# The mixer's last 512 output columns by token block in banks of their own, and routing's subtractions and the give-back matrix placed elsewhere

## The chip, the cores and the metric

One Trainium2 chip, one core. The metric is the device time of one execution in microseconds. A trace of one profiled execution is at hand; its times are counted from the start of its span. Engines: PE is TensorE (PEld its weight loads), DVE is VectorE, ACT is ScalarE, POOL is GpSimd, SP is SyncE, which here issues transfers only.

## The reference

Two blocks on 256 tokens of 1024 features, all in fp32. The first is a gated linear attention with a convolutional feed-forward. The second, where the change lies, is a token mixer (sparse attention and a gated delta rule, merged, times `w_out`), a layer norm, a mixture of 32 experts in 4 groups of 8, and a second layer norm:

```python
x = layer_norm(alpha * x + (1.0 + gt1) * y, ln_g[l, 0], ln_b[l, 0])   # y = merged @ w_out
h = x * (1.0 + sc2) + sh2
y = hier_moe(h, w_route_grp[l], w_route_exp[l], w_gate[l], w_up[l], w_down[l])
x = layer_norm(alpha * x + (1.0 + gt2) * y, ln_g[l, 1], ln_b[l, 1])

# hier_moe: the best group, in it the two best experts of 8
hb = silu(xb @ w_gate[e]) * (xb @ w_up[e])
yb = (hb @ w_down[e]) * gate
```

## The kernel before, in words

All instructions are put on the five engines' queues by a scheduler that goes by the order in which the program names them and by when they are ready in its own model; each queue then runs in order. `tc.issue_after(i)` holds what is named under it behind instruction i on i's engine.

*The mixer's output product* is `linA(xsm, w_out, ..., sink_o, tail=TAIL, fine=FINE)`. It makes two halves of 512 output columns, `ct` 0 and 1, each from four weight tiles of 256 rows. Each tile is loaded (`raw`), its high part is written by ScalarE (L177, `whi`), its low part by VectorE (L178, `wlo`); `mm3` makes three matmuls of each product (L187 to L189). With `tail=1` a tile is used for both token blocks (`tb`) of 128 as it comes. With `fine=2` the last tile of the last half is used in two steps of 256 columns for each token block. `sink_o` scales a finished piece and adds the residual (L1334, L1335), takes its statistics (L1337), and later transposes it on PE (L1343, L1344) for the routing logits (L1347); these two steps are queued behind the newest mixer matmul at that time. The slots `raw`, `lo` and `hi` (6, 4 and 4 of them) are used again for expert weights.

*Routing* is `route(tb)` for each token block: mean and scale from the statistics (`lstat`, with a power on GpSimd, L295), normalised rows `n3` and their high part `n3h` on ScalarE (L1388, L1389), and on VectorE the logits and the selection (L1383 to L1403, result `sel`), four subtractions for the low part `n3l` (L1405, one per token block and half), and the position of each token in its expert's list from a count on PE (L1410, `pos`, L1411). `onehots` compares positions (L1416, `dm`); `pick` multiplies `n3h` and `n3l` with it on PE (L1424, eight feature blocks `ff`), which collects the tokens of four experts in four banks. `gather(g)` moves these to `xg` (L1503 on VectorE, L1505 on ScalarE), then makes the gates (`gates`, L1463 to L1481), transposes `dm` to `cT` and sums each slot's gate in `gs`; these two, the give-back matrix and scale, are used when an expert's result is added to its tokens. An overflow count `nov` (L1532 to L1540) follows.

*The experts* run in 16 pairs. For each pair `gate_up` makes 64 matmuls (gate, then up), SiLU and product on ScalarE and VectorE (L1608, L1609), `turn` transposes the result, and `down` of the pair before makes 32 matmuls and gives the result back with `cT`. These matmuls go through `inorder`, which keeps them in program order on PE; a helper's line stands for all of them, L1424. `spread` (L435) makes broadcast rows on PE; those for the sums of the experts and for their scale are named in the second pair and are not held in order.

*Expert weights* are pieces of 1 MB, or of two halves, in the order of `plist`, each with a slot fixed beforehand (`cyc`); SP issues them in order (L1210), each when its slot is free. 18 pieces are named ahead of routing.

Of the kernel before, what the change touches and what calls it, by code (L numbers as in the profile page):

```python
# [9 lines left out]
F32 = mybir.dt.float32  # L10
# [11 lines left out]
CAP = 64  # L22
# [73 lines left out]
def _build(ctx, tc, nc, I, out, dbg):  # L96
# [15 lines left out]
    def bank(pool_=None, name="bank"):  # L112
        p = ps if pool_ is None else pool_
        return p.tile([128, 512], F32, tag="b", name=name)
# [71 lines left out]
    def mm3(o, ah, al, bh, bl, start, stop, **kw):  # L186
        pe.matmul(o, lhsT=ah, rhs=bh, start=start, stop=False, **kw)  # L187
        pe.matmul(o, lhsT=ah, rhs=bl, start=False, stop=False, **kw)  # L188
        mm_last[0] = pe.matmul(o, lhsT=al, rhs=bh, start=False, stop=stop, **kw).ins  # L189
# [18 lines left out]
    def linA_(xs, w, K, c0, sink, head=1, tail=1, fine=1):  # L208


        xh, xl = xs
        KT = K // 128
        for ct in range(2):
            p = [bank(pm) for _ in range(2)]

            def part(tb, k0, kn, hi, lo, cs=slice(0, 512)):
                ts = slice(tb * 128, (tb + 1) * 128)
                for k in range(kn):
                    kk = k0 + k
                    mm3(p[tb][:, cs], xh[:, kk, ts], xl[:, kk, ts], hi[:, k, cs], lo[:, k, cs], kk == 0, kk == KT - 1, skip_group_check=fine > 1)  # L220

            held = []
            tiles = [(k0, 2) for k0 in range(0, KT, 2)]
            for i, (k0, kn) in enumerate(tiles):
                held.append((k0, kn) + wload(kslice(w, k0, kn, c0 + ct * 512, 512), kn, 512))
                last = i == len(tiles) - 1
                if not last and (i < head - 1 and ct == 0 or i >= len(tiles) - tail and ct == 1):
                    yield
                    continue
                n = fine if last and ct == 1 else 1  # L230
                for tb in range(2):
                    for c in range(n):
                        cs = slice(c * 512 // n, (c + 1) * 512 // n)
                        for t in held:
                            part(tb, *t, cs)
                        if last and fine == 1:
                            sink(ct, tb, p[tb])
                        elif last:
                            sink(ct * 512 + cs.start, tb, p[tb][:, cs])
                held = []  # L240
                yield

# [42 lines left out]
                                          op1=ALU.subtract)  # L285
        return ia.ins, iv.ins

    pow_last = [None]

    def rsqrt(ms, eps, n):  # L290

        a = smp.tile([128, n], F32, tag="rs_a", name="rs_a")
        r = smp.tile([128, n], F32, tag="rs_r", name="rs_r")
        dve.tensor_scalar(out=a, in0=ms, scalar1=eps, scalar2=None, op0=ALU.add)  # L294
        pool.tensor_tensor(out=r, in0=a, in1=mhalf[:, :n], op=ALU.pow)  # L295
        return r

    def junk():
# [293 lines left out]
    with tc.tile_pool(reuse_waits="tile", name="ffn", bufs=2) as fp:  # L592
# [43 lines left out]
        for i in range(11):  # L636
            gu = {}

            def sink(nm, cw, cb):
                def f(ct, p):  # L640
                    o = fp.tile([128, 2, 256], F32, tag=nm, name=nm)
                    for c in range(2):
                        conv(p, c, i * 2 + c, cw, cb, o[:, c])
                    gu[nm] = o
                return f
# [669 lines left out]
    def mt(shape, name):  # L1315
        return mp.tile([128] + list(shape), F32, name=name, bufs=1)
# [41 lines left out]
    def lstat(st):  # L1358
        mvv = smp.tile([128, 2], F32, tag="bnmv", name="bnmv")
        dve.bn_aggr(out=mvv, in_=st)  # L1360
        return mvv[:, 0:1], rsqrt(mvv[:, 1:2], 1e-5, 1)
# [13 lines left out]
    n3h, n3l = (xtile(i, F32R, nm, (2, 2, 4, 128)) for i, nm in ((1, "n3h"), (2, "n3l")))  # L1375
    pkq = lambda ap: ap.rearrange("p (c k) -> p k c", k=4)

    def route(tb):
        m, r = lstat(lst[tb])
        nm = smp.tile([128, 1], F32, tag="nm", name="nm")  # L1380
        dve.scalar_tensor_tensor(out=nm, in0=m, scalar=-1.0, in1=r, op0=ALU.mult, op1=ALU.mult)
        l = lg[:, tb]
        dve.scalar_tensor_tensor(out=l, in0=wst[:, 0], scalar=nm, in1=wst[:, 1], op0=ALU.mult, op1=ALU.add)  # L1383
        with ExitStack():
            dve.scalar_tensor_tensor(out=l, in0=plg[tb][:, 0:36], scalar=r, in1=l, op0=ALU.mult, op1=ALU.add)

        for q, cs in enumerate(halves):
            act.activation(out=n3[:, tb, cs], in_=v3[:, tb, cs], func=AF.Identity, scale=r, bias=nm)  # L1388
            act.activation(out=n3h[:, tb, q], in_=pkq(n3[:, tb, cs]), func=AF.Copy)  # L1389

        kg, e = kg_[:, tb], el[:, tb]
        dve.tensor_reduce(out=mg_[:, tb:tb + 1], in_=l[:, 0:4], op=ALU.max, axis=AX)
        dve.scalar_tensor_tensor(out=kg, in0=l[:, 0:4], scalar=mg_[:, tb:tb + 1], in1=C("io4"), op0=ALU.is_ge, op1=ALU.mult)
        dve.tensor_reduce(out=kx[:, tb:tb + 1], in_=kg, op=ALU.max, axis=AX)
        dve.tensor_scalar(out=kg, in0=kg, scalar1=kx[:, tb:tb + 1], scalar2=-BIG, op0=ALU.is_lt, op1=ALU.mult)
        dve.tensor_tensor(out=e.rearrange("p (g e) -> p g e", g=4), in0=l[:, 4:36].rearrange("p (g e) -> p g e", g=4),
                          in1=kg[:, :, None].to_broadcast([128, 4, 8]), op=ALU.add)

        dve.max(out=m8[:, tb], in_=e)
        dve.scalar_tensor_tensor(out=ke[:, tb], in0=e, scalar=m8[:, tb, 1:2], in1=C("io32"), op0=ALU.is_ge, op1=ALU.mult)  # L1400
        dve.scalar_tensor_tensor(out=ke[:, tb], in0=e, scalar=m8[:, tb, 1:2], in1=ke[:, tb], op0=ALU.is_gt, op1=ALU.add)
        dve.max(out=k8[:, tb], in_=ke[:, tb])
        sel_last[0] = dve.tensor_scalar(out=sel[:, tb], in0=ke[:, tb], scalar1=k8[:, tb, 1:2], scalar2=None, op0=ALU.is_ge).ins  # L1403
        for q, cs in enumerate(halves):
            dve.tensor_tensor(out=n3l[:, tb, q], in0=pkq(n3[:, tb, cs]), in1=n3h[:, tb, q].bitcast(F32), op=ALU.subtract)  # L1405

        p = bank()
        if tb:
            pe.matmul(p[:, 0:32], lhsT=C("ones"), rhs=sel[:, 0], start=True, stop=False)
        i = pe.matmul(p[:, 0:32], lhsT=C("lall"), rhs=sel[:, tb], start=tb == 0, stop=True)  # L1410
        dve.scalar_tensor_tensor(out=pos[:, tb], in0=sel[:, tb], scalar=-1000.0, in1=p[:, 0:32], op0=ALU.mult, op1=ALU.add)  # L1411
        return i.ins
# [32 lines left out]
    picked = [bank(pm) for _ in range(4)]  # L1445
    route(0)
    onehots(0, 0)
    for ff in range(4):
        pick(pk(picked, ff), 0, ff, 0)
    with tc.issue_after(route(1)):  # L1450
        for ff in range(4, 8):
            pick(pk(picked, ff), 0, ff, 0)
    idm = onehots(0, 1)
    for ff in range(8):
        pick(pk(picked, ff), 0, ff, 1)

# [27 lines left out]
    def gather(g):  # L1484

        if g:
            dms[g] = dtile_()
            for tb in range(2):
                onehots(g, tb)
        dm = dms[g]  # L1490
        xg = mp.tile([128, 8, 256], F32, tag="xg", name="xg", bufs=1)
        for ff in range(8):

# [9 lines left out]
                dve.tensor_scalar(out=xg[:, ff], in0=pv, scalar1=g_, scalar2=b_, op0=ALU.mult, op1=ALU.add)  # L1503
            else:
                act.activation(out=xg[:, ff], in_=pv, func=AF.Identity, scale=g_, bias=b_)  # L1505
        if g == 0:
            with tc.issue_after(idm):
                gates()
        p, pg = bank(), bank()
        pv = p.rearrange("p (q t c) -> p q t c", q=2, t=2)  # L1510
        pgv = pg[:, 0:8].rearrange("p (q h e) -> p q e h", q=2, h=2)
# [11 lines left out]
        for e in range(2):  # L1523
            es = slice(e * 64, e * 64 + 64)
            dve.tensor_reduce(out=gs[es], in_=pgv[es, :, e], op=ALU.add, axis=AX)
        return xg, cT, gs

    NP = NE // 2
    xg, cT, gs = gather(0)

    gov = ke
    dve.tensor_scalar(out=gov, in0=pos, scalar1=CAP - 1000.0, scalar2=None, op0=ALU.is_ge)  # L1532
    dve.tensor_tensor(out=gov, in0=gov, in1=sel, op=ALU.mult)
    nov = mt([1], "nov")
    dve.tensor_reduce(out=nov, in_=gov.rearrange("p t e -> p (t e)"), op=ALU.add, axis=AX)
    p = bank()
    pe.matmul(p[0:1, 0:2], lhsT=nov, rhs=C("ones")[:, 0:2], start=True, stop=True)
    novi = mp.tile([1, 1], I32, name="novi", bufs=1)
    dve.tensor_copy(out=novi, in_=p[0:1, 0:1])
    dve.tensor_tensor(out=gov, in0=gov, in1=Gm, op=ALU.mult)  # L1540
    normT = mp.tile([16, 128], F32, name="normT", bufs=1)
    pool.dma_start(out=normT, in_=I["rows"][3072:5120].rearrange("(q c) -> q c", q=16))

    def overflow():

        def wdyn(src):
# [99 lines left out]
    def down_last(pr, hT, cT, gs):  # L1646
# [8 lines left out]
        for c in range(4):  # L1655
# [3 lines left out]
            for tb in range(2):  # L1659
                yq = yps[tb][c // 2][:, s]  # L1660
                inorder(pe.matmul, yq, lhsT=cT[:, q, tb].bitcast(F32), rhs=ye, start=False, stop=True, skip_group_check=True)
                dve.bn_stats(out=fst[tb][:, c], in_=yq)  # L1662


    todo = None
    started.append(1)
    for pr in range(NP):
        last = pr == NP - 1
        while cnt[0] < ahead[pr]:
            wpiece()  # L1670
        hs_, back = gate_up(pr, xg), (cT, gs)
        if pr == NP - 2:

            lgb = xtile(1, name="lgb", shape=(2, 1024))
            for n in range(2):
                spread_to(lgb[:, n], normT, n)
        if pr % 2 and not last:
            xg, cT, gs = gather(pr // 2 + 1)
        if pr == 1:

            yps = [[bank(pm) for _ in range(2)] for _ in range(2)]
# [45 lines left out]
RA, RB = 5, 2  # L1727
TA, TB = 1, 2
BA, AHD = (0, 2), 3
TAIL, ZH, FP_, ZP_, NB0, NB1, FINE = 1, 2, 3, 3, 10, 15, 2  # L1730

def pack(inputs):
    g = lambda n: np.asarray(inputs[n])
# [42 lines left out]
```

## Time and profile before

| | |
|---|---|
| median of three executions | 1190.06 us (1189.28 to 1191.07) |
| the profiled execution | 1189.94 us |
| its span | 1188.3 us |
| busy: PE, DVE, ACT, POOL | 1138.7, 639.2, 457.9, 56.1 us |
| from HBM | 333.12 MB read, 283 GB/s over the span |

Busy times are sums over the span; stages differ much, and PE counts as busy while its matmuls are pipelined. Start times in a timeline are of the profiled execution, in us from the span's start; a line with xN merges N instructions.

### The profile page before, as it was taken

What the parts mean: (1) busy time and instruction counts of PE and PEld (TensorE: products, weight loads), DVE (VectorE), ACT (ScalarE), POOL (GpSimd) and SP (SyncE); (2) the same over time, 40 slices, a digit from 0 to 9 for tenths busy, and PEclk for the clock granted to TensorE, in tenths of its full rate; (3) what the DMA queues carried; (4) which work ended last, traced back from release to release, by engine and by line L of the source; (5) the groups of instructions that cost most, each with busy time, mean ns of one, the idle gap of its engine ahead of it and who ended that gap; (6) DMA issues with size and microseconds to landing.
All of it is one profiled execution on the core that took longest, in us unless ns stands there. A gap on an engine that the chain in (4) does not pass through costs nothing. (4 is left out here: it accounts for less than half of the span.)

```text
span 1188.3 us, 17092 instructions
## 1 busy us (share of the span) xinstructions
PE 1138.7 (96%) x6642; PEld 806.3 (68%) x6642; DVE 639.2 (54%) x1109; ACT 457.9 (39%) x827; POOL 56.1 (5%) x76
## 2 busy tenths in 40 slices
PE   6999999999999999999999989999999799999986
PEld 5976799998778999989988765534443334434432
DVE  5797788998887899487467562212121112211104
ACT  5654566664566666453365431201010101101100
POOL 1001100000010111100100000000000000000000
PEclk9999999999999999999999989999999899999998
DMA  9884787778954647345356875999999999999992
GB/s 328 276 313 151 244 297 225 222 238 294 324 178 141 178 125 202 105 127 136 115 226 222 308 273 219 373 420 416 417 421 417 415 419 417 419 419 417 420 414 99
DMA packets 136262, 337.69 MB, mean 284 GB/s; under 512 B 12891, under 2 KB 69415, under 8 KB 121328
## 3 DMA queue, kind: packets, MB, share of 16 engines
q1 hardware_dynamic: 126160, 328.83, 75.1%
q0 software_dynamic: 1696, 5.36, 1.2%
q10 hardware_dynamic: 8320, 2.36, 0.8%
q8 instruction: 54, 0.88, 0.3%
q14 instruction: 32, 0.26, 0.1%
HBM read 333.12 MB, written 3.32 MB: 283 GB/s over the span
## 5 line engine op out<-in xcount | busy, mean ns | idle before, releaser
L178 DVE TENSOR_TENSOR wlo<-raw,whi 128x1024 fp32r<-128x1024 f32 (+1 forms) x192 | 234.0, 1222 | 81.3 <-ACT whi L177 80.4
L177 ACT ACTIVATE whi<-raw 128x1024 fp32r<-128x1024 f32 (+1 forms) x192 | 201.2, 1052 | 177.9 <-PE bank L188 65.0
L1424 PE MATMUL bank<-wmoe,xg 128*64 128x512 f32 x1024 | 233.3, 600 | 6.5 <-PEq L1553 6.1
L188 PE MATMUL bank<-xl,whi 128*128 128x256 f32 x720 | 204.6, 284 | 0.3 <-DVE xl L284 0.3
L187 PE MATMUL bank<-xh,whi 128*128 128x256 f32 x720 | 204.8, 284 | 0.0
L189 PE MATMUL bank<-xh,wlo 128*128 128x256 f32 x720 | 204.4, 284 | 0.0
L1424 PEld LDWEIGHTS bank<-wmoe,xg 128*64 128x64 f32 x1024 | 72.8, 138 | 145.3 <-issue 139.4
L188 PEld LDWEIGHTS bank<-xl,whi 128*128 128x128 f32 x720 | 137.9, 192 | 1.6 <-DVE xl L284 0.5
L187 PEld LDWEIGHTS bank<-xh,whi 128*128 128x128 f32 x720 | 138.0, 192 | 1.5 <-ACT whi L177 0.5
L189 PEld LDWEIGHTS bank<-xh,wlo 128*128 128x128 f32 x720 | 137.9, 192 | 0.9 <-issue 0.8
L1609 DVE TENSOR_TENSOR hsT<-hsT,bank 128x512 f32<-128x512 f32 x16 | 11.0, 688 | 230.7 <-PE bank L1424 217.8
L1424 PE MATMUL bank<-wmoe,hsT 128*64 128x512 f32 x480 | 112.6, 608 | 5.4 <-DMA wmoe<-in_w_down_dram 5.4
L187 PE MATMUL bank<-whi,xh 128*128 128x512 f32 (+1 forms) x276 | 108.6, 394 | 0.0
L189 PE MATMUL bank<-whi,xl 128*128 128x512 f32 (+1 forms) x276 | 106.9, 387 | 0.6 <-DVE xl L284 0.6
L188 PE MATMUL bank<-wlo,xh 128*128 128x512 f32 (+1 forms) x276 | 107.0, 388 | 0.0
L1635 ACT ACTIVATE y<-bank 128x512 fp32r<-128x512 f32 x30 | 17.9, 597 | 175.2 <-DVE bank L1633 131.3
L1424 PEld LDWEIGHTS bank<-wmoe,hsT 128*64 128x64 f32 x480 | 35.0, 140 | 74.2 <-issue 62.8
L1633 DVE SCALAR_TENSOR_TENSOR bank<-bank,gs,gt 128x512 f32<-128x512 f32 x30 | 22.8, 758 | 76.3 <-PE bank L1424 69.1
L187 PEld LDWEIGHTS bank<-whi,xh 128*128 128x128 f32 x276 | 52.6, 190 | 10.6 <-issue 1.7
L189 PEld LDWEIGHTS bank<-whi,xl 128*128 128x128 f32 x276 | 52.2, 189 | 11.1 <-DVE xl L284 1.3
L188 PEld LDWEIGHTS bank<-wlo,xh 128*128 128x128 f32 x276 | 52.4, 190 | 9.0 <-issue 0.3
L367 DVE SCALAR_TENSOR_TENSOR ada_acc<-raw_a,condT,ada_acc 128x1024 f32<-128x1024 f32 x42 | 53.6, 1276 | 0.0
(409 smaller groups left out, 1504.9 us busy)
## 6 DMA issues: line engine op xcount, KB each, us to landing
wmoe<-in_w_gate_dram SPq DMA_DIRECT2D x40, 1024.0 KB, 14.4
wmoe<-in_w_up_dram SPq DMA_DIRECT2D x40, 1024.0 KB, 14.9
wmoe<-in_w_down_dram SPq DMA_DIRECT2D x36, 1024.0 KB, 15.1
raw<-in_w_in_dram SPq DMA_DIRECT2D x62, 512.0 KB, 3.8
wmoe<-in_w_down_dram SPq DMA_DIRECT2D x56, 512.0 KB, 11.4
raw_a<-in_w_ada_dram SPq DMA_DIRECT2D x48, 512.0 KB, 4.7
wmoe<-in_w_gate_dram SPq DMA_DIRECT2D x48, 512.0 KB, 11.3
wmoe<-in_w_up_dram SPq DMA_DIRECT2D x48, 512.0 KB, 11.3
```

Source lines behind the costliest of these rows:

```text
L177: hi_last[0] = act.activation(out=hi, in_=raw, func=AF.Copy).ins
L178: lo_last[0] = dve.tensor_tensor(out=lo, in0=raw, in1=hi.bitcast(F32), op=ALU.subtract).ins
L187: pe.matmul(o, lhsT=ah, rhs=bh, start=start, stop=False, **kw)
L188: pe.matmul(o, lhsT=ah, rhs=bl, start=False, stop=False, **kw)
L189: mm_last[0] = pe.matmul(o, lhsT=al, rhs=bh, start=False, stop=stop, **kw).ins
L367: dve.scalar_tensor_tensor(out=acc, in0=raw, scalar=cs, in1=acc, op0=ALU.mult, op1=ALU.add)
L1424: i = f(*a, **k).ins
L1609: dve.tensor_tensor(out=hs_, in0=hs_, in1=gps["w_up_2"], op=ALU.mult)
L1633: dve.scalar_tensor_tensor(out=yp, in0=yp, scalar=gs[:, q:q + 1], in1=gt2[:, cs], op0=ALU.mult, op1=ALU.mult)
L1635: act.activation(out=y2[:, 0], in_=yp, func=AF.Copy)
```

## The change

The last half of the mixer's output product (`ct` 1) holds all four weight tiles (`TAIL` 4) and then runs four passes: token block 0 with its first and second 256 columns, then token block 1 likewise; each pass has a bank of its own. Of routing's four subtractions, token block 0's two are named on GpSimd, behind the power of token block 0 and of token block 1; token block 1's two stay on VectorE, one behind its selection, one behind its one-hots. Routing of token block 1 is named ahead of the first picks. `gather` is cut in two: `xg` first, and the give-back matrix and scale in `givers`. For the first four experts `gates` follows `gather`, and `givers` and the overflow count follow the first `gate_up`. The transfer of the final norm's rows (`normT`) is named later.

```diff
@@ linA_
-            p = [bank(pm) for _ in range(2)]
+            apart = fine if ct == 1 and tail >= KT // 2 else 1
+            p = [bank(pm) for _ in range(2 * apart)]
...
-                    mm3(p[tb][:, cs], xh[:, kk, ts], xl[:, kk, ts], hi[:, k, cs], lo[:, k, cs], kk == 0, kk == KT - 1, skip_group_check=fine > 1)
+                    mm3(p[tb * apart + cs.start * apart // 512][:, cs], xh[:, kk, ts], xl[:, kk, ts], hi[:, k, cs], lo[:, k, cs], kk == 0, kk == KT - 1, skip_group_check=fine > 1)
...
@@ rsqrt
-        pool.tensor_tensor(out=r, in0=a, in1=mhalf[:, :n], op=ALU.pow)
+        pow_any[0] = pool.tensor_tensor(out=r, in0=a, in1=mhalf[:, :n], op=ALU.pow).ins
...
+    def low(eng, tb, q, after):
+        with tc.issue_after(after):
+            eng.tensor_tensor(out=n3l[:, tb, q], in0=pkq(n3[:, tb, halves[q]]), in1=n3h[:, tb, q].bitcast(F32), op=ALU.subtract)
...
@@ route
+        pw = pow_any[0]
...
             act.activation(out=n3h[:, tb, q], in_=pkq(n3[:, tb, cs]), func=AF.Copy)
+            if tb == 0 and q == 0:
+                low(pool, 0, 0, pw)
+        if tb:
+            low(pool, 0, 1, pw)
...
-        for q, cs in enumerate(halves):
-            dve.tensor_tensor(out=n3l[:, tb, q], in0=pkq(n3[:, tb, cs]), in1=n3h[:, tb, q].bitcast(F32), op=ALU.subtract)
+        if tb:
+            low(dve, 1, 0, sel_last[0])
...
     onehots(0, 0)
+    i1 = route(1)
     for ff in range(4):
         pick(pk(picked, ff), 0, ff, 0)
-    with tc.issue_after(route(1)):
+    with tc.issue_after(i1):
         for ff in range(4, 8):
             pick(pk(picked, ff), 0, ff, 0)
     idm = onehots(0, 1)
+    low(dve, 1, 1, idm)
...
@@ gather
-        if g == 0:
-            with tc.issue_after(idm):
-                gates()
+        return xg
+
+    def givers(g):
+        dm = dms[g]
...
-        return xg, cT, gs
+        return cT, gs
...
-    xg, cT, gs = gather(0)
...
+    xg = gather(0)
+    gates()
...
@@ the loop over pairs
-        hs_, back = gate_up(pr, xg), (cT, gs)
+        hs_ = gate_up(pr, xg)
+        if pr == 0:
+            cT, gs = givers(0)
...
+        back = cT, gs
...
-            xg, cT, gs = gather(pr // 2 + 1)
+            xg = gather(pr // 2 + 1)
+            cT, gs = givers(pr // 2 + 1)
...
-TAIL, ZH, FP_, ZP_, NB0, NB1, FINE = 1, 2, 3, 3, 10, 15, 2
+TAIL, ZH, FP_, ZP_, NB0, NB1, FINE = 4, 2, 3, 3, 10, 15, 2
```

## Rows read from the trace of the kernel before

**Rows 1.** The page: bytes moved by slice (40 of 29.7 us), and the chain.

```profile
GB/s 328 276 313 151 244 297 225 222 238 294 324 178 141 178 125 202 105 127 136 115 226 222 308 273 219 373 420 416 417 421 417 415 419 417 419 419 417 420 414 99
...
DMA 16%; PE 3%; DVE 1%; issue 0%; DVEq 0%; ACT 0%; SPq 0%; ACTq 0%
```

**Rows 2.** Busy time by stretch; the last columns are clock, DMA share, GB/s.

```profile
720.00:725.00 5.00, 5.00 (x27) 1.94 (x28) 1.13 (x5) 0.30 (x1) 0.00 (x0) 1.00 0.04 7
...
764.00:766.00 2.00, 2.00 (x12) 0.65 (x10) 0.83 (x2) 0.60 (x1) 0.00 (x0) 1.00 0.50 188
```

**Rows 3.** Timeline of SP's queue: start, us, issues of expert weights.

```profile
705.18 0.80 SPq L1210 DMA_DIRECT2D wmoe<-in_w_down_dram  x2
...
724.04 0.80 SPq L1210 DMA_DIRECT2D wmoe<-in_w_gate_dram  x2
...
764.14 1.66 SPq L1210 DMA_DIRECT2D wmoe<-in_w_gate_dram  x3
```

**Rows 4.** Timeline of PE, the mixer's last 512 columns.

```profile
689.17 0.40 PE L187 MATMUL bank<-whi,xh 128*128 128x512 f32 x1
...
695.07 0.39 PE L189 MATMUL bank<-whi,xl 128*128 128x512 f32 x1
695.30 0.28 PE L187 MATMUL bank<-whi,xh 128*128 128x256 f32 x1
...
695.89 0.28 PE L189 MATMUL bank<-whi,xl 128*128 128x256 f32 x1
...
701.52 0.53 PE L1347 MATMUL bank<-wg,v3T 128*128 128x36 f32 x4
```

**Rows 5.** Timeline of VectorE, from the last weight tile to the second selection.

```profile
690.11 1.20 DVE L178 TENSOR_TENSOR wlo<-raw,whi 128x1024 fp32r<-128x1024 f32 x1
...
705.24 0.15 DVE L294 TENSOR_SCALAR rs_a<-bnmv 128x1 f32<-128x1 f32 x1
...
712.79 0.24 DVE L1403 TENSOR_SCALAR sel<-ke,k 128x32 f32<-128x32 f32 x1
```

**Rows 6.** Timeline of PE, from the picks to the second pair.

```profile
713.90 0.41 PE L1424 MATMUL bank<-dm,n3l 128*128 128x256 f32 x1
714.11 0.41 PE L1424 MATMUL bank<-dm,n3h 128*128 128x256 f32 x1
...
717.63 0.28 PE L1424 MATMUL bank<-dm,n3l 128*128 128x256 f32 x1
717.75 0.49 PE L1424 MATMUL bank<-cst,dm 128*128 128x128 f32 x3
718.17 1.60 PE L435 MATMUL bank<-rowsT,cst 48*128 48x128 f32 x12
...
720.36 4.94 PE L1424 MATMUL bank<-wmoe,xg 128*64 128x512 f32 x22
...
734.24 1.16 PE L435 MATMUL bank<-rowsT,cst 48*128 48x128 f32 x8
...
754.66 3.90 PE L435 MATMUL bank<-rowsT,cst 48*128 48x128 f32 x28
```

**Rows 7.** Groups of instructions by line and shape, VectorE: busy us, mean ns.

```profile
L178 DVE TENSOR_TENSOR wlo<-raw,whi 128x1024 fp32r<-128x1024 f32 x188 | 231.3, 1234 | 78.7 <-ACT whi L177 77.8
...
L654 DVE TENSOR_TENSOR hl<-g,hh 128x512 fp32r<-128x512 f32 x11 | 7.5, 684 | 0.0
...
L1405 DVE TENSOR_TENSOR n3l<-v,n3h 128x512 fp32r<-128x512 f32 x4 | 4.3, 1077 | 0.5 <-ACT n3h L1389 0.5
```

**Rows 8.** Timeline of all engines around 473 us.

```profile
473.40 1.28 POOL L1017 TENSOR_TENSOR am<-AT,cst 128x512 f32<-128x512 f32 x1 [3.67 <-DMA scr<-am]
473.41 2.36 DVE L178 TENSOR_TENSOR wlo<-raw,whi 128x1024 fp32r<-128x1024 f32 x1
```

**Rows 9.** Busy time by stretch, two stretches of PE's granted clock.

```profile
707.00:708.00 1.00, 0.00 (x0) 0.00 (x0) 1.00 (x3) 1.00 (x3) 0.00 (x0) 0.50 0.91 369
...
757.00:758.00 1.00, 1.00 (x9) 1.00 (x8) 0.00 (x0) 0.60 (x1) 0.00 (x0) 0.69 1.04 426
```

More of the change, by code (lines that the diff above doesn't have):

```diff
@@ L238, in linA_ @@
                         elif last:
-                            sink(ct * 512 + cs.start, tb, p[tb][:, cs])
+                            sink(ct * 512 + cs.start, tb, p[tb * apart + cs.start * apart // 512][:, cs])
                 held = []
@@ L286, in tsplit_block @@
         return ia.ins, iv.ins
-    pow_last = [None]
+    pow_last, pow_any = [None], [None]
     def rsqrt(ms, eps, n):
@@ L1383, in route @@
         dve.scalar_tensor_tensor(out=l, in0=wst[:, 0], scalar=nm, in1=wst[:, 1], op0=ALU.mult, op1=ALU.add)
-        with ExitStack():
-            dve.scalar_tensor_tensor(out=l, in0=plg[tb][:, 0:36], scalar=r, in1=l, op0=ALU.mult, op1=ALU.add)
+        dve.scalar_tensor_tensor(out=l, in0=plg[tb][:, 0:36], scalar=r, in1=l, op0=ALU.mult, op1=ALU.add)
         for q, cs in enumerate(halves):
@@ L1489, in gather @@
                 onehots(g, tb)
-        dm = dms[g]
         xg = mp.tile([128, 8, 256], F32, tag="xg", name="xg", bufs=1)
@@ L1525, in gather @@
             dve.tensor_reduce(out=gs[es], in_=pgv[es, :, e], op=ALU.add, axis=AX)
-        return xg, cT, gs
+        return cT, gs
     NP = NE // 2
-    xg, cT, gs = gather(0)
[L1531 to L1542, printed above, removed]
+    xg = gather(0)
+    gates()
     def overflow():
@@ L1662, in down_last @@
                 dve.bn_stats(out=fst[tb][:, c], in_=yq)
+    normT = mp.tile([16, 128], F32, name="normT", bufs=1)
+    pool.dma_start(out=normT, in_=I["rows"][3072:5120].rearrange("(q c) -> q c", q=16))
     todo = None
@@ L1670, in _build @@
             wpiece()
-        hs_, back = gate_up(pr, xg), (cT, gs)
+        hs_ = gate_up(pr, xg)
+        if pr == 0:
+            cT, gs = givers(0)
+            gov = ke
+            dve.tensor_scalar(out=gov, in0=pos, scalar1=CAP - 1000.0, scalar2=None, op0=ALU.is_ge)
+            dve.tensor_tensor(out=gov, in0=gov, in1=sel, op=ALU.mult)
+            nov = mt([1], "nov")
+            dve.tensor_reduce(out=nov, in_=gov.rearrange("p t e -> p (t e)"), op=ALU.add, axis=AX)
+            p = bank()
+            inorder(pe.matmul, p[0:1, 0:2], lhsT=nov, rhs=C("ones")[:, 0:2], start=True, stop=True)
+            novi = mp.tile([1, 1], I32, name="novi", bufs=1)
+            dve.tensor_copy(out=novi, in_=p[0:1, 0:1])
+            dve.tensor_tensor(out=gov, in0=gov, in1=Gm, op=ALU.mult)
+        back = cT, gs
         if pr == NP - 2:
```

## The prediction

> **What bounds the kernel now.** I read the page's slices and chain first, then busy time by stretch, the DMA queue's timeline, and last the engines' timelines between the mixer's output product and the first expert. The GB/s row falls to 219 in slice 24 (713 to 743 us), is 373 in slice 25, and then stays between 414 and 422 until slice 38; the chain that ended last is made of transfers of expert weights [rows 1]. So the last 450 us run at the pace of the transfers, and time is won or lost only where the transfers stand still before that. The reader is to see two such places. The first: the last pieces loaded ahead are issued at 705.18, the next at 724.04, and from 720 to 725 the DMA engines are 4% busy [rows 2, 3]. The next pieces wait for a slot that the first expert's gate matmuls free: those begin at 720.36, sixteen of them free two slots [rows 3, 6]. The second, small: from 764 to 766 the share is 0.50; what ends it is the issue at 764.14, which waits for slots that the first down product frees [rows 2, 3]. Since the transfers ran dry there once, an earlier start of the first gate matmuls doesn't reach the end by itself: the first down product must come earlier too. After it there is no gap, and any shift of that product goes unchanged to the end.
>
> **The change, part by part.**
>
> *The mixer's last 512 columns.* Before, three of the four weight tiles run 512 columns wide: 27 starts from 689.17 to 695.07 are 0.227 us apart; the last tile's 256-wide ones are 0.118 apart (six starts, 695.30 to 695.89) [rows 4]. Now all are 256 wide: 36 at 0.227 (8.17) become 72 at 0.118 (8.50): +0.3 us. A pass over one token block and half now needs the fourth tile after 18 matmuls, 2.1 us after the stage's start near 686.6 and the four transposes in it, so near 689.3; but its low part is written from 690.11 to 691.31 [rows 5], because the sums of the first 512 columns stand ahead of it on VectorE. That is a hole of 2.0 us. The second half has a bank of its own and its 18 matmuls over tiles one to three (2.1 us) fit the hole, so I take 0; if the queue is not so ordered it costs 2.0.
>
> What the order buys: token block 0 is summed about 5 us earlier. But its routing logits end with a product that is queued behind the last mixer matmul of all, as now (701.52) [rows 4]. So its selection can't start earlier; only its mean, scale, normalised rows and their high parts come out of the way (four small VectorE instructions, about 0.7 us).
>
> The low and high slots of the four weight tiles are also slots for expert pieces. Before they come free tile by tile, as the 512-wide matmuls go on; now all at the end, near 700. Nine half pieces and two whole ones (6.5 MB) then wait on SP's queue, which is in order; at the 417 GB/s of rows 1 they land by about 717, while the next slots come free near 718 (724.04 less the 5.8 us below). Cost 0, cover of about 1 us; if they were later, the pieces behind them would be by as much.
>
> *Routing's subtractions.* Four of 1.077 us [rows 7] stand in VectorE's queue between the two selections: token block 1's scale waits until 705.24 and its selection ends with 712.79 [rows 5]. Now two go to GpSimd and two behind that selection: -4.3 us on it, and -0.7 from above.
>
> Against it: the second GpSimd subtraction starts right after token block 1's power on GpSimd, just when both selections run. A GpSimd product of the same size took 1.28 us at 473.40; a VectorE subtraction with both inputs in SBUF that began with it took 2.36 instead of its mean of 1.23 [rows 7, 8], so it stood still for 1.13. The read here is strided; on VectorE that makes 0.684 into 1.077 [rows 7], so GpSimd's may take 1.28 x 1.57 = 2.0. Bounds of the wait: 0, if the small instructions of a selection pass, and 2.0. Nearest row: 1.13; I take 1.3. The first GpSimd subtraction falls in the mixer's last passes, where VectorE has slack: 0.
>
> The Trainium skill's page "SBUF — State Buffer", section "Who interferes with whom", says that a VectorE instruction with two SBUF inputs contends with GpSimd's reads and that the later one is blocked for the whole instruction, whatever its size; by that the lower bound 0 falls away and the sum stays as it is. No row of before shows it for a small instruction.
>
> Sum for token block 1's selection: 0.3 - 4.3 - 0.7 + 1.3 = -3.4. Behind it one subtraction (1.08) now stands before the position sum, where PE's count needs some 0.7 anyway: +0.4 on the one-hots, but PE still has token block 0's picks to do there, so it is covered. The 24 picks after the count end at 717.75; the first are 0.21 apart (713.90, 714.11), the last 0.12, and the granted clock was 0.50 before them, at 707 to 708 [rows 6, 9]. I keep their length and give 0.1 for the last subtraction. Picks end -3.3, near 714.5.
>
> *The give-back matrix and the overflow count.* Before, the last pick is followed by transposes, 12 filler matmuls (broadcast rows for the sums, 718.17) and the give-back products until 720.36 [rows 6]; the gates for them wait for VectorE's evictions. Now the gate matmuls follow the picks at once, as each of their eight steps needs one eviction alone: -2.5, so the first gate matmul comes at -5.8, about 714.5. The moved work (about 1.1 us of PE) falls into the 1.1 us in which PE waited for the first product of SiLU and up, from 734.24 on, filled before by 8 more fillers [rows 6]: 0. If that wait is gone, it costs 1.1.
>
> But the 20 fillers must run somewhere before the first down product, and there the other 28 already stand in one string (754.66, 3.90 us) [rows 6]. At that spacing they cost 20 x 0.131 = 2.6; in that string the clock fell (mean 0.69 from 757 to 758) [rows 9], and by the picks' ratio (0.21 to 0.12) they would cost 4.6 at half clock. I take 3.2, nearer the row.
>
> *The row constants' transfer* moves behind GpSimd's subtractions; it is read in the last but one pair: 0. *Tracing routing of block 1 before the first picks* changes no work; if PE's queue then held those picks back behind the second count, it would cost eight picks, 1.7 at 0.21 each.
>
> **Sum.** First gate matmul -3.3 - 2.5 = -5.8; first down product -5.8 + 3.2 = -2.6; the transfers after it and the end: -2.6. The profiled execution took 1189.94 (span 1188.3 and 1.64 around it), so 1187.3; the median, 1190.06, lies 0.12 above that execution, so I say 1187.5. From its bounds (wait 0 to 2.0, fillers 2.6 to 4.6) this case alone runs from -0.4 to -4.5; its likely part is 1186 to 1189. What a measurement of this kernel can tell from no change is about 0.2%, 2.4 us.
>
> **The rivals.**
>
> *More comes through.* If the selections' small instructions pass beside GpSimd (+1.3 gained) or the fillers find idle places as before (+3.2), the time is 1186.2 or 1184.3. For it: the scheduler did place 20 of 48 in gaps. Against: both gaps are used up by the change.
>
> *PE stands still in the first pass.* If the queue holds the passes one after another, the 2.0 us hole is real and only -0.6 is left: 1189.5. For it: the low part's end at 691.31 is fixed by VectorE's queue. Against: matmuls of other products are woven into this stage already.
>
> *GpSimd is the wrong engine.* Its subtraction takes 2.0 and both selections wait for all of it: -1.9, 1188.2. The Trainium skill's "GPSIMD Engine Reference", section "Engine selection", gives elementwise work on a tile to VectorE, since GpSimd is about 2x slower with two inputs; by its ratio the estimate is 2.1 us, and the sum would be -1.8. The rows have 1.28 against 0.684, a ratio of 1.9, without a stride.
>
> *The transfers hide it.* If the pieces loaded ahead, now later, end after the slots come free by all that was won, the end stays: 1190.1. Against: 1 us of cover by the rate above.
>
> *Slower: the clock.* The picks now come in shorter bursts behind the count and two late subtractions. If the clock is still at half when the gate matmuls begin, each costs as much as 0.2 us more. From 13 of them on nothing is won; from 25 on it is over 0.2% slower, 1192.5 or more. Against: the clock came back during the picks, and in the string at 754.66 soon after it.
>
> **How the numbers follow.** Chances: the forecast 0.45, more 0.20, PE's hole 0.15, GpSimd 0.05, hidden 0.05, clock 0.10. Faster by over 0.2%: all of "more" and 0.30 of the forecast, which lies across that line: 0.50. Within 0.2%: the forecast's other 0.15 and 0.25 of the next three: 0.40. Slower: 0.10. The range leaves out the clock case above and the best half of "more" below: 1185.0 to 1190.4.
>
> **What would show it.** First gate matmul near 714.5, and before it no give-back products; 48 fillers in one string before the first down product, and that one near 755.9; VectorE's small instructions with pauses of over 1 us when the second GpSimd subtraction runs; first pass with 18 matmuls of the second half in its middle; transfers at full rate from the down product on. Wrong it would be if the gain at the gate matmuls and at the end were the same, if PE waited in the mixer, or if the granted clock were 0.5 past the first gate matmuls.

## The result, and the profile after

The changed kernel took 1197.58 us (median of five, 1195.43 to 1198.69), the kernel before 1190.06 (five, 1188.92 to 1192.17): a ratio of 1.0052, 95% interval 1.003 to 1.0073. The forecast was 1187.5 and the range ended at 1190.4: outside it, and on the other side. The experiments below show that this difference isn't the change's. Executions of either kernel come in two groups about 10 us apart, with or without a stretch at half clock near 480 us, far ahead of the change; all five of the changed kernel here fell into the one (their mean granted clock is 0.977 to 0.980, that of the profiled execution of the kernel before is 0.985) and all five of the kernel before into the other. Like with like, the change gains 2 to 4 us.

First the page of the changed kernel: TensorE's granted clock and the bytes moved, by slice of 29.9 us (counted from 0, as in the prediction), and the chain that ended last.

```profile
PEclk9999999999999999699999998999999899999998
...
GB/s 328 285 297 165 250 288 229 219 235 311 311 172 131 184 119 222 42 136 118 133 172 235 320 173 341 342 416 417 417 420 417 416 419 415 421 418 417 420 414 112
...
PE 11%; DMA 9%; DVE 1%; issue 0%; DVEq 0%; ACT 0%; SPq 0%; ACTq 0%
```

The transfers still run at 414 to 421 GB/s, from slice 26 to 38 [rows 1 for before]. The chain now has more of TensorE (11% of the span, 3% before) than of transfers (9%, 16% before): the two take turns in it. But slice 16 (478 to 508 us) has 42 GB/s, and its clock digit is 6. The same 20 us by busy time (columns: PE, PEld, DVE, ACT, POOL, clock, DMA share, GB/s), first before, then after:

```profile
480.00:500.00 20.00, 20.00 (x164) 19.43 (x164) 8.87 (x16) 9.32 (x23) 3.54 (x4) 1.00 0.22 69
```

```profile
480.00:500.00 20.00, 20.00 (x96) 20.00 (x96) 2.63 (x7) 2.66 (x8) 3.23 (x4) 0.50 0.01 4
```

TensorE is busy all the time in both, but does 96 matmuls in place of 164: the granted clock is 0.50, the 1.2 GHz level. TensorE's timelines, before and after, from the delta rule, which the diff doesn't touch, to the first transposes of the attention branch's end, and behind them the first down product before and the logits' last-queued product after:

```profile
478.40 1.06 PE L1006 MATMUL bank<-cst,Tm 128*128 128x128 f32 x8 [2.09 <-DMA Tm<-scr]
479.30 1.90 PE L1022 MATMUL bank<-Tm,am 128*128 128x64 f32 x16
481.03 1.06 PE L1029 MATMUL bank<-TT,X 128*128 128x64 f32 x8
...
670.14 0.60 PE L280 MATMUL bank<-cst,mg 128*128 128x128 f32 x4
...
758.49 8.21 PE L1424 MATMUL bank<-wmoe,hsT 128*64 128x512 f32 x32
```

```profile
477.60 1.06 PE L1008 MATMUL bank<-cst,Tm 128*128 128x128 f32 x8 [2.29 <-DMA Tm<-scr]
478.50 2.70 PE L1024 MATMUL bank<-Tm,am 128*128 128x64 f32 x16
480.99 1.91 PE L1031 MATMUL bank<-TT,X 128*128 128x64 f32 x8
...
679.10 0.60 PE L282 MATMUL bank<-cst,mg 128*128 128x128 f32 x4
...
710.68 0.53 PE L1349 MATMUL bank<-wg,v3T 128*128 128x36 f32 x4
```

The reader is to see: TensorE waits some 2 us for a transfer in both; after it the same products of 64 columns take 1.91 in place of 1.06; and the changed kernel, 0.8 us ahead at that wait, is 8.96 behind at 670. Up to there every queue stands in the same order in both kernels. So the time at the first transposes (670.14, 679.10) is the zero for all that the change did:

| from the first transposes | before | after | difference |
|---|---|---|---|
| logits' product behind the last mixer matmul | 31.38 | 31.58 | +0.2 |
| block 0's selection | 38.30 | 38.35 | 0.0 |
| block 1's selection | 42.65 | 40.97 | -1.7 |
| first gate matmul | 50.22 | 46.90 | -3.3 |
| first down product | 88.35 | 86.91 | -1.4 |
| end of the span | 518.16 | 516.80 | -1.4 |

The span's +7.6 is +8.96 - 1.36. The rows behind the lower lines of the table: VectorE in routing before, then of the changed kernel VectorE, GpSimd and ScalarE.

```profile
703.56 0.15 DVE L1393 SCALAR_TENSOR_TENSOR kg__7350<-lg,mg__7349,cst 128x4 f32<-128x4 f32 x1
704.18 1.09 DVE L1405 TENSOR_TENSOR n3l<-v,n3h 128x512 fp32r<-128x512 f32 x1 [0.47 <-ACT n3h L1389]
...
706.07 0.16 DVE L1381 SCALAR_TENSOR_TENSOR nm<-bnmv,rs_r 128x1 f32<-128x1 f32 x1 [0.47 <-POOL rs_r L295]
...
706.95 1.06 DVE L1405 TENSOR_TENSOR n3l<-v,n3h 128x512 fp32r<-128x512 f32 x1
...
708.44 0.24 DVE L1403 TENSOR_SCALAR sel<-ke,k 128x32 f32<-128x32 f32 x1
```

```profile
712.21 1.37 DVE L1404 SCALAR_TENSOR_TENSOR kg__7388<-lg,mg__7387,cst 128x4 f32<-128x4 f32 x1
...
714.61 1.46 DVE L1389 SCALAR_TENSOR_TENSOR nm<-bnmv,rs_r 128x1 f32<-128x1 f32 x1 [0.54 <-POOL rs_r L297]
...
717.45 0.23 DVE L1414 TENSOR_SCALAR sel<-ke,k 128x32 f32<-128x32 f32 x1
...
720.07 0.24 DVE L1414 TENSOR_SCALAR sel<-ke,k 128x32 f32<-128x32 f32 x1
720.22 1.10 DVE L1383 TENSOR_TENSOR n3l<-v,n3h 128x512 fp32r<-128x512 f32 x1
```

```profile
712.02 1.53 POOL L1383 TENSOR_TENSOR n3l<-v,n3h 128x512 fp32r<-128x512 f32 x1 [6.11 <-ACT n3h L1396]
714.02 0.56 POOL L297 TENSOR_TENSOR rs_r<-rs_a,mhalf 128x1 f32<-128x1 f32 x1 [0.46 <-DVE rs_a L296]
714.53 1.52 POOL L1383 TENSOR_TENSOR n3l<-v,n3h 128x512 fp32r<-128x512 f32 x1
```

```profile
710.82 1.13 ACT L1396 ACTIVATE n3h<-v 128x512 fp32r<-128x512 f32 x1 [1.73 <-PE bank L188]
```

Two instructions on 1 and 4 elements a partition, block 1's `nm` and block 0's `kg`, take 1.46 and 1.37 us in place of 0.16 and 0.15: each begins 0.1 to 0.2 us after a GpSimd subtraction and ends with it. The first GpSimd subtraction waited 6.11 us for n3h, whose write waited for TensorE (a product of line 188, the mixer's): n3h is put where the mixer's inputs lie until its last matmul.

TensorE from the first pick to the first down product, changed kernel:

```profile
719.11 0.58 PE L1435 MATMUL bank<-dm,n3h 128*128 128x256 f32 x1 [0.31 <-DVE dm L1427]
719.49 0.42 PE L1435 MATMUL bank<-dm,n3l 128*128 128x256 f32 x1
719.70 0.41 PE L1435 MATMUL bank<-dm,n3h 128*128 128x256 f32 x1
...
725.80 0.28 PE L1435 MATMUL bank<-dm,n3l 128*128 128x256 f32 x1
...
726.00 13.95 PE L1435 MATMUL bank<-wmoe,xg 128*64 128x512 f32 x64
739.89 0.66 PE L1435 MATMUL bank<-cst,dm 128*128 128x128 f32 x4
740.30 0.59 PE L1435 MATMUL bank<-Gp,dm 128*128 128x4 f32 x4
...
740.94 0.71 PE L437 MATMUL bank<-rowsT,cst 48*128 48x128 f32 x4
...
760.90 5.17 PE L437 MATMUL bank<-rowsT,cst 48*128 48x128 f32 x44
766.01 8.78 PE L1435 MATMUL bank<-wmoe,hsT 128*64 128x512 f32 x32
```

And the two places where transfers stand still, by busy time and on SP's queue [rows 2, 3]:

```profile
726.00:731.00 5.00, 5.00 (x25) 1.78 (x26) 1.73 (x8) 1.96 (x3) 0.00 (x0) 1.00 0.39 133
...
771.00:773.00 2.00, 2.00 (x12) 0.66 (x10) 0.86 (x2) 0.60 (x1) 0.00 (x0) 1.00 0.08 33
```

```profile
729.68 7.67 SPq L1212 DMA_DIRECT2D wmoe<-in_w_gate_dram  x4
...
774.82 5.50 SPq L1212 DMA_DIRECT2D wmoe<-in_w_up_dram  x3
```

The first place is shorter than before (a DMA share of 0.39 over 5 us, for 0.04), the second deeper (0.08, for 0.50): this fits the prediction, by which an earlier start of the gate matmuls alone doesn't reach the end.

### The profile page after: what moved, and what is told of

Same layout as the page of the kernel before. It is cut to its first block, busy times and chain, and to the rows that moved or that the text cites. A ratio compares the mean times of both kernels' runs of the same rounds, so it can differ in the third digit from the quotient of the medians.

```text
span 1195.9 us, 17166 instructions
## 1 busy us (share of the span) xinstructions
PE 1146.8 (96%) x6678; PEld 816.6 (68%) x6678; DVE 639.8 (53%) x1107; ACT 458.3 (38%) x827; POOL 58.6 (5%) x78
```

## The experiments

Differences of medians are in us, with 95% intervals from drawing the executions anew. Three chips took part in four sets (experiment 1; 2 to 4 on the same chip; 5; 6); in each set the kernel before ran beside.

**1. Both kernels unchanged, and the change in two parts.** The routing part alone keeps `TAIL` at 1 in the changed kernel; the mixer part alone is the kernel before with `linA`'s banks and `TAIL = 4`.

> The kernel before, unchanged, timed as a kernel of its own. Its last matmul of the attention branch ends at 670 us, that of the changed kernel at 679 us, though up to there both have the same instructions in the same order on every engine; the changed kernel's granted clock was 0.50 from 479.4 to 499.9 us. Theory A (coincidence): whether the clock falls in that stretch of the delta rule has nothing to do with the change, so some of these executions show a mean clock near 0.977 and 1196 to 1198 us, the others 0.985 and 1189 to 1192. Theory B (the changed program brings it): every execution here has a mean clock near 0.985 and 1188 to 1192 us.

> The changed kernel, unchanged, again. Theory A: some executions without the half-clock stretch near 480 us, these at 1187 to 1190 us with a clock near 0.985 (the change by itself gains 1.4 us between 679 and the end). Theory B: all at a clock of 0.976 to 0.981 and 1195 to 1199 us.

> The changed kernel with TAIL 1: the mixer's last half as before, all of the routing and give-back edits kept. From the end of the attention branch to the first down product: I expect 0.5 to 2 us less than before, as the subtractions leave VectorE's queue in front of the second selection. Upstream: theory A, the half-clock stretch in some executions, as in any kernel; theory B, it is there in all or in none, and tells whether the mixer's part is needed for it.

> The kernel before with the mixer's four passes alone (TAIL 4, a bank for each). From the end of the attention branch to the first down product: between 0.5 us more and 0.5 us less than before, since the routing logits of token block 0 still end behind the last pass. Upstream as in the run with the routing edits alone: theory A, some executions with the half-clock stretch; theory B, all or none.

Medians: 1192.07, 1190.76, 1188.99, 1194.76 (12 executions each; ratios to the kernel before 0.9983, 0.9972, 0.998, 0.9983, each within 0.993 to 1.002: by themselves they tell nothing). But the executions lie in two groups, here called the lower and the upper one: in the 35 of the kernel before beside them 17 from 1185.9 to 1193.6, 18 from 1196.9 to 1207.3, and the changed kernel's six from 1185.1 to 1187.0 and six from 1194.5 to 1200.2. The two profiles fell the other way round than the recorded ones, by busy time, kernel before and then changed kernel:

```profile
480.00:500.00 20.00, 20.00 (x98) 20.00 (x99) 2.63 (x7) 2.82 (x8) 3.58 (x4) 0.52 0.00 0
```

```profile
480.00:500.00 20.00, 20.00 (x164) 19.42 (x163) 8.88 (x16) 9.92 (x30) 2.81 (x4) 1.00 0.21 56
```

Their spans are 1195.5 and 1183.5. So the stretch comes and goes with the same kernel. In the lower groups the medians are 1189.90 (kernel before, 24), 1185.87 (changed), 1188.35 (routing alone, 8) and 1188.40 (mixer alone, 6): the change -4.0 (-5.2 to -2.6), its parts -1.6 (-2.6 to -0.3) and -1.5 (-2.7 to +1.4), the last not clear of zero.

By the profiles, from the first transposes to the first down product, the routing part alone takes 86.93 us, as expected less than before (88.35 here, 88.76 to 89.10 in four further profiles). That is already what the whole change takes (86.83 to 86.92). The mixer part alone takes 87.70, earlier by more than the 0.5 us expected; beside the routing part it adds nothing there. With the routing part alone GpSimd costs in other places: its first subtraction ran ahead of block 1's power on GpSimd, so that `nm` waited 2.12 us for it (0.47 before), and the second stopped the one-hots (1.10 us in place of 0.42).

**2. TensorE's wait filled.** In both kernels:

```
+            for _ in range(18 if hg == 0 and tb == 0 else 0):
+                with tc.issue_after(mm_last[0]):
+                    pe.transpose(h4(p)[:, 0], ident, ident)
             for h in range(4):
                 with tc.issue_after(mm_last[0]):
                     pe.transpose(h4(p)[:, h], Tm[:, tb, h], ident)
```

and `NB0` 13 in place of 10, so that the other matmuls woven in there come ahead of the fillers.

> The kernel before with 18 transposes of the identity on TensorE ahead of the transposes of Tm, to fill its wait of 2.1 us for the transfer of Tm. Theory A (the granted clock falls in that wait in some executions and not in others, and that is the 9 us): the clock is 1.00 from 478 to 500 us, the executions fall into one group near those of before without the stretch, median 1189.5 (1188 to 1191.5), none over 1195. Rival (the two groups have another cause, and the half clock only goes with it): two groups stay, some executions at 1197 to 1202.

> The changed kernel with the same 18 transposes. Theory A: one group, median 1186 (1184.5 to 1187.5), so the change by itself is worth -2 to -4 us against the kernel before with the same fillers, -0.2 to -0.35%. Rival (the change itself costs time, and its fast executions were chance): within 1 us of the kernel before with the fillers, or slower than it.

Measured 1189.86 (1188.65 to 1193.21) and 1185.78 (1184.14 to 1189.31). TensorE of the kernel before with fillers, then busy time of the changed one:

```profile
478.21 2.13 PE L1006 MATMUL bank<-cst 128*128 128x128 f32 x18
480.18 1.04 PE L1009 MATMUL bank<-cst,Tm 128*128 128x128 f32 x8
```

```profile
480.00:500.00 20.00, 20.00 (x164) 19.41 (x164) 8.93 (x16) 8.77 (x16) 3.54 (x4) 1.00 0.18 55
```

No execution of either lies in the upper group; of the 33 of the unchanged kernel before beside them 17 do. Over all kernels with these fillers (here and below) it is 1 of 100, without them 72 of 150 (kernel before) and 12 of 24 (changed). So theory A (the clock falls in that wait in some executions of either kernel) is shown: with the wait filled the 10 us are gone, in both kernels. Fillers and `NB0` were changed together, and no run says which of them is needed. Nor does the wait's length by itself decide: in the eight profiles without fillers it is 2.02 to 2.29 us where the clock fell behind it and 2.09 to 2.53 where it held. And the change by itself: -4.1 (-6.2 to -2.1).

**3. What the stops beside GpSimd cost.** The changed kernel with the fillers; GpSimd's two subtractions left out, so that the low part of token block 0 is missing from the picks:

```
-        for i, n in enumerate((n3h, n3l)):
+        for i, n in enumerate((n3h, n3l if tb else n3h)):
```

> The one before it without GpSimd's two subtractions: the picks of token block 0 take the high part twice instead of high and low, so the low part of block 0 is left out of the result. Lock theory (VectorE's two stops of 1.2 and 1.3 us beside GpSimd keep the first gate matmul back): block 1's selection and the first gate matmul both 2.5 us earlier, counted from the first transposes of the attention branch (46.9 us from there to the gate matmul in both profiles of the changed kernel). Clock theory (the 32 picks run one behind the other at half clock from block 0's selection on, so only what lies ahead of that counts): block 1's selection 2.5 us earlier, the first gate matmul 1.2 us (45.7 us).

```profile
703.98 0.16 DVE L1391 SCALAR_TENSOR_TENSOR nm<-bnmv,rs_r 128x1 f32<-128x1 f32 x1 [0.53 <-POOL rs_r L297]
...
705.83 0.23 DVE L1412 TENSOR_SCALAR sel<-ke,k 128x32 f32<-128x32 f32 x1
```

The instruction that took 1.46 takes 0.16 again, and the first gate matmul comes 44.40 us after the first transposes, against 46.67: -2.27. It is the lock theory's figure, by another path: block 0's selection itself comes 2.2 us earlier (36.19 us against 38.35 in the kernel with the fillers alone, from the first transposes), because both stops stand ahead of it on VectorE. The profile's span is 2.7 us shorter, but the median hardly moved: 1185.23, -0.5 (-2.8 to +0.6), an interval that holds both the profile's gain and none.

**4. Routing's waits filled too.** Twelve transposes between the last logits, 28 products of 256 columns on n3h ahead of block 0's count, and the count of block 1 named behind the first picks.

> The changed kernel with the 18 transposes and with 12 transposes and 28 products of 256 columns in TensorE's waits of routing, between the mixer's last matmul and block 0's selection. Clock theory: the clock stays at 1.00, a pick takes 0.12 us in place of 0.21, the picks end with block 1's last low part: first gate matmul 1.4 to 2.6 us earlier than in the changed kernel, the end as much, median 1184 (1183 to 1185.5). Lock theory: the picks wait for block 1's selection and its low part anyway, the gate matmul moves by less than 0.5 us, and the median is that of the changed kernel with the 18 transposes alone.

1188.50: +2.7 (+0.9 to +3.9) on the same kernel without. The edit had a side effect; TensorE's first pick:

```profile
711.63 0.39 PE L1451 MATMUL bank<-dm,n3h 128*128 128x256 f32 x1 [2.61 <-DVE dm L1443]
```

It waits 2.61 us (0.31 in the changed kernel): the scheduler had put the gates' small instructions ahead of block 0's positions on VectorE. So this run tells neither theory; with `gates()` held behind block 1's one-hots it was repeated below.

**5. A second wait upstream, and the two costs of routing.** Five profiles of kernels without the whole change had the clock at half for 3.4 to 6.8 us from 136 or 137 us on, the five with it not. `tsplit_block` got the same kind of fillers there (18 and 3), in four kernels; the third has all four subtractions on VectorE (`low(dve, ...)` behind block 0's selection, behind its one-hots, and twice behind block 1's one-hots), the fourth repeats 4.

> The kernel before with the delta rule's 18 transposes and with 21 more in TensorE's waits of 2.25 and 0.39 us for xn near 135 us, where the five profiles of kernels without the whole change have the clock at half for 3.4 to 6.8 us and the five with it don't. If that stretch is part of the 4.1 us between the two kernels with the delta rule's fillers (theory U, upstream), this kernel gains 1 to 1.5 us on the one without the 21: median 1188.5, and its first transposes of the attention branch come as early as the changed kernel's. If not (theory D, all of it comes behind the mixer), the median stays at 1189.9.

> The changed kernel with the same 39 transposes. Both theories: median 1185.8 (1184.5 to 1187), as with the 18 alone. Theory U: 2.5 to 3 us under the kernel before with the same 39, theory D: 4 us under it.

> The one before it with all four low parts on VectorE: block 0's first half right behind block 0's selection, its second behind block 0's one-hots, block 1's two behind block 1's one-hots. Leaving GpSimd's two out brought the first gate matmul 2.3 us forward. Lock theory: the same gain less 0.2 us (block 0's positions wait for the rest of one subtraction) and less about 0.6 us (block 1's picks wait for their low part): gate matmul 1.2 to 1.8 us earlier than in the one before it, median 1184.5. Rival (VectorE's own time is as dear as the stops were, as in the kernel before): gate matmul and median within 0.5 us of the one before it.

> The 39 transposes and the fillers in routing's waits once more, with the gates' small instructions kept behind block 1's one-hots, so that block 0's positions no longer stand behind them on VectorE (2.3 us in the run with fillers there). Clock theory: picks at 0.12 us a product, first gate matmul 1.2 to 2.5 us earlier than in the changed kernel with the 39, median 1184. Lock theory: less than 0.5 us earlier, since block 1's selection and low parts end last.

Medians: 1189.95 (one of its twelve, 1200.35, is in the upper group after all), 1187.92, 1186.37, 1185.57. None of the four profiles has the stretch at 136. Against the same kernels without the second fillers, which ran on another chip, the first two fit neither theory: the kernel before gained nothing, the changed one lost 2.1, so the change is worth -1.9 here (-3.7 to -0.4, without the 1200.35). In the third the gate matmul comes at 45.48 against 45.97 in the second (-0.5: the rival's figure) and the median is -1.5 (-3.3 to +1.4), which doesn't decide. The fourth held the clock, as busy time from 704 to 716 shows, second kernel and then fourth:

```profile
704.00:716.00 12.00, 7.42 (x40) 6.93 (x41) 10.50 (x42) 5.79 (x12) 3.56 (x3) 0.72 1.02 384
```

```profile
704.00:716.00 12.00, 10.99 (x88) 10.11 (x88) 11.17 (x41) 6.93 (x13) 3.60 (x3) 1.00 1.02 386
```

Gate matmul at 44.51 (-1.5), first down product 84.51 against 86.92, median -2.3 (-3.2 to -0.5): the clock theory's figures for the gate matmul, though its median of 1184 was not reached. Of the 1.5 us 1.3 lie in the picks, which take 4.4 us in place of 5.7 from first to last. The further 0.9 at the down product is the second kernel's clock, at half for 6.8 us from 756 on; the four other profiles of the changed kernel have the gate matmul at 46.67 to 46.91 and the down product at 86.83 to 86.91, so the fourth kernel is 2.2 to 2.4 ahead of them at both. No run has the fillers without the gates' later place.

**6. Both kernels once more, and both costs away.** The third is the last kernel with the four subtractions on VectorE and 10 products in place of 28.

> The kernel before, unchanged, once more. Theory A: two groups of executions, near 1190 and near 1200 us, both present. Rival (the change moves the kernel from one group into the other): nearly all near 1190.

> The changed kernel, unchanged, once more. Theory A: two groups, near 1186 and near 1196 us, each about 4 us (1.9 to 4.1) under the group of the kernel before. Rival: nearly all near 1196.

> The changed kernel with the 39 transposes upstream, the fillers of routing (10 products in place of 28, since block 0's selection now comes 2.3 us sooner), the gates behind block 1's one-hots and all four low parts on VectorE. If the stops beside GpSimd and the half clock add up: first gate matmul 0.5 to 1.2 us earlier than with GpSimd's two (44.5 us from the first transposes of the attention branch), median 1184.8 (1183.5 to 1186). If the two subtractions on VectorE take back what the stops cost once the picks run at full clock: gate matmul at 44.5 or later, median 1185.5 or above.

The kernel before: 8 executions up to 1191.4, 4 from 1197.7; the changed one: 6 from 1184.7 to 1187.5, 6 from 1195.2 to 1200.5. Theory A again, on a third chip. All unchanged executions together, 24 against 150: without the stretch 1185.92 and 1189.87, -3.9 (-4.7 to -3.0); with it 1197.25 and 1200.37, -3.1 (-4.8 to -1.5), without three of the kernel before over 1204. This time it is the changed kernel's profile that has the stretch at 136 (136.71) and the other's that has none, so that pattern was chance. The third: gate matmul at 45.34, 1186.13 (1183.92 to 1188.18): no better than with GpSimd (1185.57, on another chip). But its picks didn't run at full clock: TensorE waited 1.19 us for block 1's selection, and from 710.2 us on the granted clock was 0.50 for 3.4 us. So this run doesn't tell what two subtractions on VectorE cost beside picks at full clock.

## Why the prediction was wrong

**The step that failed first is the sum's last: "so 1187.3".** It was made against one execution's time as if all that stands ahead of the mixer were fixed. It isn't: the wait for Tm's transfer, in both kernels, ends with the clock at half or not, and that is 10 us. No rival had it; the one on the slower side looked for half clock behind the change, at the gate matmuls, where the profile after shows 1.00 (726 to 731). The 0.2% that the prediction took for the least difference to be told came from three executions, all of the lower group. The profile of one execution can't show this, but it could have warned: a wait of 2.09 us for a transfer, ahead of a chain that TensorE alone sets.

**What bounds the end: right.** In five profiles of each kernel, fillers or not, the time from the first down product to the span's end is 426.8 to 429.9 us, with a mean of 428.1 for either; the end moved by what that product moved (-1.4 and -1.4). This shows the shift, and not that the transfers alone set the pace behind it, since TensorE has its share in the chain.

**The mixer: right.** +0.2 on its last matmul for a forecast of +0.3, and no hole: other products filled it. The -0.7 for the small instructions out of the way is nearly there, too: with the mixer part alone block 0's and block 1's selections come 0.5 and 0.6 earlier (37.76 and 42.06).

**Picks end -3.3: wrong, -0.8** (last pick 725.80 less 679.10, against 717.63 less 670.14 [rows 6]). Two terms failed. "The first GpSimd subtraction falls in the mixer's last passes, where VectorE has slack: 0" cost 1.2: its n3h can't be written before the mixer's inputs are dead, so it came out in the middle of block 0's selection. The second cost 1.3, as forecast, but block 1's `nm` stands ahead of block 0's remaining steps on VectorE, so both delay block 0: its selection stayed where it was (0.0). The prediction had all four subtractions between the two selections; two of them stood ahead of block 0's (704.18, 706.95), and without them and without the stops it comes 2.1 earlier (36.19 in experiment 3, and block 1's 4.1 earlier, 38.52, for the -4.7 of the prediction's terms without GpSimd). The stops took that back. And "I keep their length" took block 1's selection as what releases the picks; with that one 1.7 earlier, the 32 products ran one behind the other from 719.11, 0.21 apart at half clock for 6.0 of their 6.7 us, and their start hangs on block 0. The Trainium skill's page "SBUF — State Buffer", section "Who interferes with whom", had it that VectorE's later instruction is blocked for GpSimd's whole one, whatever its size: the trace agrees (0.16 became 1.46, 0.15 became 1.37), and the lower bound of 0 is gone.

**Give-back moved, -2.5: right, -2.5** (gate matmul -3.3 less the picks' -0.8).

**The fillers, +3.2: too dear, +1.3; the moved give-back work, 0: too cheap, +0.6.** From the first gate matmul to the string of fillers it is 34.90 us (760.90 less 726.00), before 34.30 [rows 6]: the moved work and four of the 48 fillers, which found a place behind it, took 0.6 more than the wait that they fill. The string takes 5.11 us up to the first down product, before 3.83 (758.49 less 754.66): +1.3, less than the low end of 2.6. It grew by 16 and not by 20 (28 to 44), at 5.17 / 44 = 0.117 us each, full clock; before, the clock fell at its end [rows 9]. Where it didn't, in four further profiles of the kernel before, it is 37.6 us from the gate matmul to the down product in place of 38.13, for 40.00 in three of the changed one: +2.4 there, of which the 16 fillers are 1.9.

**GpSimd the wrong engine.** A strided subtraction takes 1.53 there and 1.10 on VectorE, a ratio of 1.4; the estimate of 2.0 by the stride was too high. For this strided read so was the ratio of about 2 of the Trainium skill's page "GPSIMD Engine Reference", section "Engine selection"; without a stride the rows of before have 1.9 [rows 7, 8]. Its price here is the stop that it makes on VectorE, and what stands behind that stop.

**Together**: -5.8 + 3.2 = -2.6 forecast, -3.3 + 1.9 = -1.4 in the recorded pair of profiles. Four further profiles of the kernel before have 88.76 to 89.10 us to the first down product in place of 88.35 (half clock 3.4 us longer in the picks), four of the changed one 86.83 to 86.92: there it is -2.1. The medians of like executions say -1.9 to -4.1. So the size forecast for the change itself stands within what was measured, and only the sign on record doesn't. That the size fits is in part luck: in the recorded pair the picks gave 2.5 less than forecast, and the way from the gate matmul to the down product cost 1.3 less. (By the prediction's own bounds its weakest case is -0.5, not -0.4.)

**Open.** What decides in an execution whether the clock falls. Why all five executions of the one recorded kernel had the stretch and none of the other: with even chances that is 2 in 1024. In all six later timings of kernels without fillers both groups occur among the twelve, so either the five and five were chance or they shared something that no run shows. And why the medians give up to 2 us more than the profiles' -2.1; the spans scatter by 1 to 2 us behind the down product, too, with half clock near 1115 or 1155 in some.

## What to carry to other kernels

Compare executions only after reading the granted clock stretch by stretch: a 2 us wait of TensorE in code that nobody touched can outweigh the change more than twice over, and 18 transposes of no use otherwise in it, with more of other work woven in ahead of them, are worth more (10 us in half of the executions) than the change (2 to 4). Before an engine is relieved by another, ask when the other's input is free to be written, and what small instructions stand beside it. Where work is moved off a selection, look which selection the next queue starts from: an earlier second one gives nothing while the first one's products still run.

## What was not expected of the hardware

- The same kernel, chip and data give two groups of executions about 10 us apart; the half-clock stretch near 480 us lasted 20.48 us in two profiles, 23.89 in a third, 3.41 in a fourth, whose first transposes come at 671.19 us (668.89 to 670.74 in those without the stretch), and was absent in the other four without fillers. It follows TensorE's wait for a transfer in each.
- TensorE fell to half clock in routing in every profile without fillers there (6.8 to 13.7 us). 12 transposes and 28 products, with the gates' small instructions out of the way, kept it at 1.00, which was worth 2.3 us at the median. With a wait left behind the fillers (2.61 us in experiment 4, 1.19 in the last kernel) it still fell, for 3.4 us.
